# A two-layer hybrid block on one core: x loaded ahead of the weights, recurrence gates in four 64x64 quadrants, and a planner with a refitted GpSimd clock

## The chip, the cores and the metric

The kernel runs on one core of one Trainium2 chip, as one program and one launch. The metric is the time of an execution in microseconds (us), the median of several. The engines are TensorE (PE for its matmuls, PEld for its weight loads), VectorE (DVE), ScalarE (ACT), GpSimd (POOL) and SyncE (SP), which issues most of the DMAs. Each engine takes its own instructions in the order in which the program lists them, and waits on semaphores for the others. The program is laid out ahead of time: what stands in front of what on each engine is fixed when the kernel is built.

## The reference

The input is a latent stream `x` (256 tokens by 1024), 256 context tokens, two conditioning vectors, and the weights of two layers, all in float32. Each layer modulates both streams, multiplies them by one large input matrix, runs four token mixers on the result, merges their outputs, and ends with a convolutional feed-forward part.

```python
for i in range(DEPTH):                       # two layers
    mod_l = silu(c) @ w_mod[i] + b_mod[i]    # the same for the context
    zl = split_cols(modulate(x, sh1, sc1) @ w_in[i])
    zc = split_cols(modulate(h_ctx, csh1, csc1) @ w_in[i])
    ret_c, ret_l = retention(zc, zl)
    hg_c, hg_l   = hgrn2(zc, zl)
    gd_c, gd_l   = gdn(zc, zl)               # a unit lower triangular solve per 64-token chunk
    lr_c, lr_l   = rglru(zc, zl)
    y_l = merge([ret_l, hg_l, gd_l, lr_l], zl['merge_gate'])
    x = layernorm(alpha * x + g1 * y_l)
    x = layernorm(alpha * x + g2 * conv_ffn(modulate(x, sh2, sc2)))
    # the context stream does the same in every layer but the last

def rglru_direction(xc):                     # xc: conv of 512 channels, 8 blocks of 64
    r  = sigmoid(einsum('btnk,nkj->btnj', xb, w_a) + b_a)
    gi = sigmoid(einsum('btnk,nkj->btnj', xb, w_i) + b_i)
    a  = exp(-8 * r * softplus(-lam))
    h_t = a_t * h_{t-1} + sqrt(1 - a_t**2) * gi_t * xc_t
```

The recurrence's gate matrices `w_a` and `w_i` are block diagonal: 8 blocks of 64 by 64.

## The kernel before, in words

The class `Net` writes the program. Weights stream from memory in 512 KB tiles (`wraw`, issued on SP); ACT rounds each to a high part `wH` and DVE or POOL computes the low part `wL`, so that float32 products are made of matmuls named by target: `gft` and `gtf` for the input, merge and down projections, `up` for the feed-forward part, `mg_b` for the branches. `modp` matmuls make the modulation vectors from `wraw` tiles; each result row is copied by ACT (`modrow`), turned into columns by PE (`modcp`) and used as scale and shift.

The mixers are written as Python generators ("threads"). A thread yields the engine that its next step starts on and the tiles which that step needs. Two or three lanes per layer run them one behind another: the gated delta rule (`gdn0`, `gdn1`, tiles named `gd_...`) and HGRN2 (`hg_...`) in one, the recurrence (`lru_...`) and retention (`ret_...`) in another. `ro_t` are transposes of a mixer's readout. Beside them runs the stream of projection matmuls, called gemm below.

What comes next in the program is chosen by a planner. Every written instruction is charged a modelled duration on a modelled clock of its engine (`account`, L170 on), and `pump` (L302 on) takes, again and again, the candidate with the earliest modelled start: the next step of a thread, at the time at which its tiles are ready by those clocks, or the next gemm step. So a thread's step stands on PE behind as much gemm work as the planner believes will cover the wait for its input. If the input comes later than believed, PE stands still there, since the order is fixed.

The change touches four places. **The head** (`body`): the constants `ck`, then `ctx`, then `x` are loaded through ACT's queue while SP's queue loads weight tiles; `modulate` normalises both streams (row statistics, normalised `x`, transposes `xmt`, scale and shift into `xmH` and a float32 copy `xm`, low part `xmL`). **The gates** (`lru`): for each of 4 channel blocks `b` and 2 directions `d`, two matmuls of a 128x128 weight (two 64x64 blocks on its diagonal, the rest zero) against `xc` [128, 512]. A float32 matmul is two records in the trace. **The triangular solve** (`blocks`, `prep`): PE transposes `gd_Bt`, DVE masks it, SP stores 32x32 blocks to `blk` in memory and loads them as `gd_z` [64, 1024]; POOL then runs a serial substitution of 60 small operations, called the chain below; SP stores the result to `blk` and loads it back as `gd_Z`; DVE and ACT copy it into `gd_T`; PE goes on with the transposes `gd_Tt`. There are four chains, two per layer. **The planner's numbers**: POOL's cost and the placing of what follows.

Of the kernel before, what the change touches and what calls it, by code (L numbers as in the profile page):

```python
# [45 lines left out]
SUBST = 2.0  # L46
X32_BIAS = 99
LEAD = dict(PE=0.3, ACT=0.5, DVE=0.5, POOL=0.5, SP=0.0)
LN_FIRST = 1.0

EVAC_FIRST = 2.0
# [72 lines left out]
class Net:  # L124
# [36 lines left out]
    def account(self, key, name, a, k):  # L161
        dma = name == "dma_start"
        out = k.get("out", a[0] if a else None)
        if dma:
            ins = [k.get("in_", a[1] if len(a) > 1 else None)]
        else:
            ins = [x for x in a[1:] if isinstance(x, bass.AP)] + [x for n, x in k.items() if n != "out" and isinstance(x, bass.AP)]
        n = 1
        for st, c in out.ap[1:]:
            n *= c  # L170
        c = self.clk
        on, inn = self.names(out), [y for x in ins for y in self.names(x)]
        t = max([c[key]] + [max(self.base.get(x, 0.0), self.after(self.rd, x, key)) for x in on] + [self.after(self.rdy, x, key) for x in inn])
        if not dma:

            for x in ins:
                if x.space == PSUM:
                    t = max([t] + [e for p, e in self.rd.get(x.tensor.name, {}).items() if p != key])
        by = key
        if DEBUG and key == "PE":  # L180
            cand = [(c[key], "self")] + [(self.base.get(x, 0.0), "slot " + x) for x in on] + [(e + LAT[p][key], p + " rd " + x) for x in on for p, e in self.rd.get(x, {}).items()]
            cand += [(e + LAT[p][key], p + " " + x) for x in inn for p, e in self.rdy.get(x, {}).items()]
            self.dbg_t = (t, max(cand)[1].rsplit("_", 1)[0])
        if key == "PE":
            up = lambda z: 32 if z <= 32 else 64 if z <= 64 else 128
            mode = up(ins[0].ap[0][1]), up(out.ap[0][1])
            if name == "transpose":
                d = 0.11
            elif ins[0].dtype == F32R:
                mode = 128, 128  # L190
                d = (n if n >= 256 else 4 * n) / 2400.0 + 0.0135
            else:
                d = max(4 * n / 2400.0, 0.2) + 0.01
                if out.ap[0][1] == 32:
                    d *= 0.28
            if mode != self.mode:

                self.mode = mode
                d += 0.095
            d = self.clocked(t, d)  # L200
        elif dma:
            if key == "POOL":
                c[key] = t + 1.04
            else:
                self.hw = max(t + 0.05, self.hw) + 0.45
                c[key] = self.hw
            d = out.ap[0][1] * n * 4 / DMA_RATE
            t = max(c[key] + 0.7, c["DMA"])
            c["DMA"] = t + d
            by = "DMA"  # L210
        elif key == "ACT":
            d = 0.1 + n / 1200.0 + 0.07 * max(0, len(ins) - 1)
            need = {AF.Tanh: "exp", AF.Exp: "exp", AF.Ln: "ln", AF.Sqrt: "sqrt"}.get(a[2])
            if need not in (None, self.table) and not (a[2] == AF.Exp and self.table == "ln"):
                self.table = need
                t = max(t, c[key] + 1.28)
        elif key == "DVE":
            sc = [x for x in ins[1:] if len(x.ap) == 2 and x.ap[1][1] == 1]
            e = n * 1.04e-3
            src_ps = any(x.space == PSUM for x in ins)  # L220
            if name in ("tensor_scalar", "tensor_copy") and not src_ps:
                e *= 0.5
            if name == "copy_predicated":
                e = n * 1.13e-3
            if name == "reciprocal":
                e *= 6
            if name == "tensor_tensor_scan":
                e = n * 2.1e-3
            if name == "tensor_reduce" or name.startswith("bn"):
                m = 1  # L230
                for st, cc in ins[0].ap[1:]:
                    m *= cc
                e = m * 1.04e-3
            d = 0.07 + e + 0.06 * len(sc)
            if self.port_op(name, ins, sc):
                t = self.port(key, t, d)
        else:
            d = 0.14 + n * 2.1e-3
            t = self.port(key, t, d)
        if not dma:  # L240
            c[key] = t + d
        for x in on:
            q = self.rdy.setdefault(x, {})
            q[by] = max(q.get(by, 0.0), t + d)
        for x in inn:
            q = self.rd.setdefault(x, {})
            q[by] = max(q.get(by, 0.0), t + d)
# [56 lines left out]
    def pump(self, until):  # L304

        while not until():
# [3 lines left out]
            for n, x in enumerate(self.threads):  # L310
                e, r = self.when(x)
                if r is not None:
                    c.append((max(self.clk[e], r) - LEAD[e] - (x[3] if r <= self.clk[e] and e != "PE" else 0.0), n))
            if g is not None and (not c or min(c)[0] > g):
                self.gemm_step()
                continue
# [564 lines left out]
    def modulate(self, i, half, sg, xs):  # L881
# [26 lines left out]
        for d in range(0, 8, 2):  # L908
# [12 lines left out]
            for q in range(2):  # L921
                A.activation(H[:, q, :], z[q], AF.Identity, scale=sc[q], bias=sh[q])
            for q in range(2):
                if self.clk["ACT"] + X32_BIAS < self.clk["DVE"]:
                    A.activation(x32[:, q, :], z[q], AF.Identity, scale=sc[q], bias=sh[q])
                else:
                    V.tensor_scalar(x32[:, q, :], z[q], sc[q], sh[q], op0=ALU.mult, op1=ALU.add)
# [79 lines left out]
    def body(self):  # L1007
# [13 lines left out]
        f0 = self.fa = self.fb = self.pool("f0", "right")  # L1021
        self.fw = self.pool("fw")
        xs = {}
        self.A.dma_start(self.ck, self.I["c_f32"])
        for sg, nm in ((0, "ctx"), (1, "x")):
            xs[sg] = self.tile(f0, [128, 2, 1024], F32, "f_r", "x0", 2)
            self.A.dma_start(xs[sg], self.I[nm][0].rearrange("(j p) d -> p j d", p=128))
        self.feed()
        ts = [self.spawn(self.modulate(0, 0, sg, [xs[sg][:, j, :] for j in range(2)])) for sg in range(2)]
        ct = self.spawn(self.derive())  # L1030
# [460 lines left out]
    def lru(self, inst):  # L1491
# [17 lines left out]
        for b in range(4):  # L1509
            yield lambda: inst["jobs"][2 * b].done  # L1510
            xc, w = inst["xc"][b], inst["w"][b]
            yield [xc, w]
            T = self.tile(self.l2, [128, 2, 512], F32, "lT", "lru_T", 1)
            As, XIs = [], []
            for d in range(2):
                th = []
                for ty in range(2):
                    ps = self.pmt([128, 512], "lru_gp")
                    mm(ps, w[:, d * 2 + ty, :], xc, start=True, stop=True)
                    t = self.tile(self.l2, [128, 512], F32, "lt", "lru_t", 2)  # L1520
                    hb = pd["hb"][:, ty * 8 + d * 4 + b:ty * 8 + d * 4 + b + 1]
                    A.activation(t, ps, AF.Tanh, scale=0.5, bias=hb)
# [9 lines left out]
                As.append(a_)  # L1532
                XIs.append(xi)
                if d == 0:
                    yield [xc]
            yield "ACT", [T]
            A.activation(T, T, AF.Sqrt, scale=-0.25)
            yield "DVE", [T]
# [378 lines left out]
    def gdn(self, inst, g):  # L1917
# [144 lines left out]
        def prep(seg, R):  # L2062
# [8 lines left out]
                self.S.dma_start(Z[:, :, w, :], self.diag(1, seg, w))  # L2071
            for z in (T, TT):
                V.memset(z[:, :, 0, :], 0.0)
            yield "DVE", [Z, TT, T]
            for b in range(4):
                ps = slice(32 * b, 32 * b + 32)
                V.tensor_copy(TT[ps, :, 0, ps], Z[ps, :, 0, :])
# [205 lines left out]
def _host_arrays(a, specs):  # L2283
    f = np.float32
    out = {}
# [11 lines left out]
    for i in range(DEPTH):  # L2297
# [19 lines left out]
        for d in range(2):  # L2317
            for ty, nm in enumerate(("lru_w_a", "lru_w_i")):
                for bk in range(4):
                    for q in range(2):  # L2320
                        lruw[i, 64 * q:64 * q + 64, bk, d * 2 + ty, 64 * q:64 * q + 64] = a[nm][i, d, 2 * bk + q]
    out["bm"] = a["b_mod"].reshape(DEPTH, 12, 512)
    out.update(par=par, parf=parf, nw=nw, rows=rows, lruw=lruw)
    out.update(_constants())
# [31 lines left out]
```

## Time and profile before

| | |
|---|---|
| median of 3 runs | 2199.26 us (2198.85 to 2202.68) |
| profiled execution: its own time | 2195.15 us |
| profiled execution: span from first to last instruction | 2193.4 us |
| PE busy | 2023.3 us (92%) |
| DVE busy | 1478.5 us (67%) |
| ACT busy | 849.5 us (39%) |
| POOL busy | 436.4 us (20%) |
| mean TensorE clock granted | 0.967 of full speed |

PE is the engine that is hardly ever free: the span less its busy time leaves 170 us. Idle time of the other engines costs nothing by itself; it matters where PE waits for them. Times in the rows are microseconds from the start of the span. Since matmul ends are modelled and pipelined, the distance from one start to the next says more than the duration of one.

### The profile page before, as it was taken

How to read it: one execution, taken by the hardware profiler on the slowest of the kernel's cores; microseconds unless marked ns; L12 is line 12 of the kernel's file. 1: busy time of each engine (PE TensorE's matmuls, PEld its weight loads, DVE VectorE, ACT ScalarE, POOL GpSimd, SP SyncE). 2: the span in 40 equal slices, each digit the busy share in tenths (PEclk: the TensorE clock that was granted, in tenths of full speed). 3: DMA queues.
4: the chain of work that ended last, by engine and by line, in shares of the span. 5: the costliest groups of instructions: out<-in, count | busy, mean ns of one | idle time of the engine just before them, and what ended most of it. 6: DMA issues, size and time to landing. Idle time of an engine off the chain costs nothing. (4 is left out here: it accounts for less than half of the span.)

```text
span 2193.4 us, 34754 instructions
## 1 busy us (share of the span) xinstructions
PE 2023.3 (92%) x13820; PEld 1752.4 (80%) x13820; DVE 1478.5 (67%) x2491; ACT 849.5 (39%) x1259; POOL 436.4 (20%) x440
## 2 busy tenths in 40 slices
PE   5998999999999999779999997999989899888997
PEld 3676777788888878678898876788988799878996
DVE  5785665445737457986636678896584566878786
ACT  3354431322332333344423433566332333325553
POOL 0273216111101101220000022282127112301000
PEclk9999999999999999989999998999999899988999
DMA  7453434434341457553233244354433322575553
GB/s 264 130 160 100 158 112 149 134 109 142 102 150 62 159 192 254 184 192 116 92 102 97 96 149 160 126 179 133 140 107 110 112 81 75 177 272 211 181 185 115
DMA packets 128963, 316.22 MB, mean 144 GB/s; under 512 B 28928, under 2 KB 51232, under 8 KB 128800
## 3 DMA queue, kind: packets, MB, share of 16 engines
q1 hardware_dynamic: 127280, 308.96, 43.0%
q0 software_dynamic: 832, 2.54, 0.3%
q8 instruction: 109, 1.79, 0.3%
q10 hardware_dynamic: 688, 2.49, 0.3%
q14 instruction: 54, 0.44, 0.1%
HBM read 290.84 MB, written 23.10 MB: 143 GB/s over the span
## 5 line engine op out<-in xcount | busy, mean ns | idle before, releaser
L91 DVE TENSOR_TENSOR wL<-wraw,wH 128x1024 fp32r<-128x1024 f32 (+1 forms) x326 | 405.5, 1250 | 154.7 <-ACT wH L91 154.5
L91 ACT ACTIVATE wH<-wraw 128x1024 fp32r<-128x1024 f32 (+2 forms) x391 | 401.7, 1032 | 233.9 <-PE gtf L91 146.0
L91 POOL TENSOR_TENSOR wL<-wraw,wH 128x1024 fp32r<-128x1024 f32 (+1 forms) x65 | 148.2, 2284 | 1131.6 <-ACT wH L91 1078.5
L91 PE MATMUL gft<-xmH,wH 128*128 128x512 f32 x512 | 211.0, 412 | 0.8 <-ACT wH L91 0.8
L91 PE MATMUL gft<-xmL,wH 128*128 128x512 f32 x512 | 203.4, 397 | 3.7 <-DVE xmL L91 3.7
L91 PE MATMUL gft<-xms,wH 128*128 128x256 f32 x1344 | 186.6, 290 | 4.2 <-ACT wH L91 4.1
L91 PEld LDWEIGHTS gft<-xms,wH 128*128 128x128 f32 x1344 | 170.5, 193 | 11.5 <-issue 5.0
L91 DVE SCALAR_TENSOR_TENSOR ffy<-up,parf,ffy 128x255 f32<-128x255 f32 (+1 forms) x188 | 110.8, 590 | 71.3 <-ACT ffy L91 65.5
L91 PE MATMUL up<-xmL,wH 128*128 128x512 f32 (+1 forms) x400 | 146.9, 374 | 6.9 <-DVE xmL L91 6.9
L91 PE MATMUL up<-xmH,wH 128*128 128x512 f32 (+1 forms) x400 | 146.0, 372 | 5.1 <-ACT wH L91 2.8
L91 PE MATMUL gft<-xmH,wL 128*128 128x512 f32 x512 | 132.8, 398 | 0.0
L91 PEld LDWEIGHTS gft<-xmH,wH 128*128 128x128 f32 x512 | 97.5, 190 | 28.9 <-issue 8.6
L91 PE MATMUL gtf<-wH,xmH 128*128 128x256 f32 (+1 forms) x384 | 110.2, 314 | 9.0 <-DVE gy L91 7.5
L91 ACT ACTIVATE ffy<-up,parf 128x256 f32<-128x256 f32 (+1 forms) x94 | 61.3, 652 | 145.7 <-PE up L91 145.6
L91 PEld LDWEIGHTS gft<-xmL,wH 128*128 128x128 f32 x512 | 97.7, 191 | 23.6 <-DVE xmL L91 5.3
L91 PE MATMUL gtf<-wH,hidH 128*128 128x256 f32 (+1 forms) x352 | 114.3, 341 | 2.3 <-DVE gy L91 1.7
L91 PE MATMUL gtf<-wH,hidL 128*128 128x256 f32 (+1 forms) x352 | 113.9, 340 | 0.0
L91 PEld LDWEIGHTS gft<-xmH,wL 128*128 128x128 f32 x512 | 95.5, 190 | 20.0 <-issue 0.3
L91 PE MATMUL gtf<-wH,xmL 128*128 128x256 f32 (+1 forms) x384 | 105.7, 302 | 0.0
L91 PE MATMUL gft<-xms,wL 128*128 128x256 f32 x672 | 95.8, 288 | 6.1 <-DVE wL L91 6.1
L91 PE MATMUL up<-xms,wH 128*128 128x256 f32 x704 | 94.0, 287 | 5.1 <-DVE xms L91 3.8
L91 PEld LDWEIGHTS up<-xmL,wH 128*128 128x128 f32 x400 | 78.6, 197 | 20.1 <-DVE xmL L91 8.3
(330 smaller groups left out, 4272.9 us busy)
## 6 DMA issues: line engine op xcount, KB each, us to landing
wraw<-in_wt SPq DMA_DIRECT2D x466, 512.0 KB, 3.7
thd<-mg_t SPq DMA_DIRECT2D x32, 256.0 KB, 2.3
mg_th<-thd SPq DMA_DIRECT2D x32, 256.0 KB, 3.1
lnw<-in_rows SPq DMA_DIRECT2D x8, 512.0 KB, 7.1
thd<-mg_t SPq DMA_DIRECT2D x32, 128.0 KB, 2.6
xmm<-thd SPq DMA_DIRECT2D x16, 256.0 KB, 5.5
wraw<-in_wt SPq DMA_DIRECT2D x14, 256.0 KB, 2.6
brd<-ro_b SPq DMA_DIRECT2D x28, 128.0 KB, 1.9
```

The lines of the kernel that those rows point to most:

```text
L91: r = f(*a, **k)
```

## The change

First, in the head, `ctx` is loaded by SP ahead of the weight tiles, `x` is the first load on ACT's queue, and `ck` comes behind it. In the first `modulate` the float32 copies `xm` may be made by ACT where its modelled clock is behind DVE's, which puts one of each two on ACT.

Second, in `lru`, ACT makes `xs`, a copy of `xc` with its two halves of 64 partitions exchanged (two activations of [64, 512] per `b`, 16 in all). The two gates of a direction are then four matmuls of a 64x64 weight block against 64 partitions of `xc` or `xs`, one for each quadrant of the 128x128 array, in place of two matmuls of 128x128. The packed weights of the second gate are exchanged to match. There are 64 such matmuls of 64x512 in place of 32 of 128x512.

Third, the planner: POOL's modelled cost changes from 0.14 + 2.1e-3 n to 0.22 + 2.0e-3 n (n elements per partition), a step that begins on PE is placed 0.8 us later outside the head (`PE_MARGIN`), and the copies behind a chain are placed 2 us later (`CHAIN_LAG`). A 64x64 matmul is charged 0.27 of its former cost.

```diff
+PE_MARGIN = 0.8
+CHAIN_LAG = 2.0
...
                 if out.ap[0][1] == 32:
                     d *= 0.28
+                elif out.ap[0][1] == 64 and ins[0].ap[0][1] == 64:
+                    d *= 0.27
...
-            d = 0.14 + n * 2.1e-3
+            d = 0.22 + n * 2.0e-3
...
-                    c.append((max(self.clk[e], r) - LEAD[e] - (x[3] if r <= self.clk[e] and e != "PE" else 0.0), n))
+                    m = PE_MARGIN if e == "PE" and r > self.clk[e] - PE_MARGIN and not self.head else 0.0
+                    c.append((max(self.clk[e], r + m) - LEAD[e] - (x[3] if r <= self.clk[e] and e != "PE" else 0.0), n))
...
-                if self.clk["ACT"] + X32_BIAS < self.clk["DVE"]:
+                if self.clk["ACT"] + (0.0 if first else X32_BIAS) < self.clk["DVE"]:
...
+        for sg, nm, q in ((0, "ctx", self.S), (1, "x", self.A)):
+            xs[sg] = self.tile(f0, [128, 2, 1024], F32, "f_r", "x0", 2)
+            q.dma_start(xs[sg], self.I[nm][0].rearrange("(j p) d -> p j d", p=128))
         self.A.dma_start(self.ck, self.I["c_f32"])
-        for sg, nm in ((0, "ctx"), (1, "x")):
-            xs[sg] = self.tile(f0, [128, 2, 1024], F32, "f_r", "x0", 2)
-            self.A.dma_start(xs[sg], self.I[nm][0].rearrange("(j p) d -> p j d", p=128))
...
-            yield [xc, w]
+            xs = self.tile(self.l2, [128, 512], F32, "lxs", "lru_xs", 1)
+            yield "ACT", [xc, xs]
+            for q in range(2):
+                A.activation(xs[64 * q:64 * q + 64, :], xc[64 - 64 * q:128 - 64 * q, :], AF.Copy)
+            yield [xs, w]
...
+                pp = [self.pmt([128, 512], "lru_gp") for _ in range(2)]
+                for q in range(2):
+                    for ty, z in enumerate((xc, xs)):
+                        o0, i0 = 64 * q, 64 * (q ^ ty)
+                        mm(pp[ty][o0:o0 + 64, :], w[i0:i0 + 64, d * 2 + ty, o0:o0 + 64], z[i0:i0 + 64, :], start=True, stop=True)
                 for ty in range(2):
-                    ps = self.pmt([128, 512], "lru_gp")
-                    mm(ps, w[:, d * 2 + ty, :], xc, start=True, stop=True)
+                    ps = pp[ty]
...
-            yield "DVE", [Z, TT, T]
+            yield "DVE", [Z, TT, T], "free", CHAIN_LAG
...
-                        lruw[i, 64 * q:64 * q + 64, bk, d * 2 + ty, 64 * q:64 * q + 64] = a[nm][i, d, 2 * bk + q]
+                        r = 64 * (q ^ ty)
+                        lruw[i, r:r + 64, bk, d * 2 + ty, 64 * q:64 * q + 64] = a[nm][i, d, 2 * bk + q]
```

The three pieces below show how the written order moves. The first is the start of ACT's program, before and after; `ck`, `x_118` (context) and `x_120` (latents, `x_119` after) are the loads named above.

```order
L91 ACTIVATE cth<-c_91 128x16
L91 DMA ck<-in_c_f 128x768
L91 DMA x_118<-in_ctx 128x2x1024
L91 DMA x_120<-in_x 128x2x1024
L91 ACTIVATE sp_e_141<-sp_ax_140 128x8
```

After the change the same engine begins:

```order
L94 ACTIVATE cth<-c_91 128x16
L94 DMA x_119<-in_x 128x2x1024
L94 DMA ck<-in_c_f 128x768
L94 ACTIVATE sp_e_141<-sp_ax_140 128x8
L94 ACT_TABLE_LOAD
```

`x` has moved from third to first on this queue. The load of the context has gone from it and stands on SP between `par` and the first `wraw`.

The second place is PE at the end of the first chain of layer 0, from the last gemm matmuls ahead of `gd_Tt` on; `gd_Y`, `gd_X` and `gd_XT` are the next steps of the same solve. Before:

```order
L91 MATMUL gft<-xmL,wH 128x512
L91 MATMUL gd_Tt<-ck,gd_T 128x128 x8
L91 MATMUL gft<-xmH,wH 128x512
L91 MATMUL gft<-xmL,wH 128x512
L91 MATMUL gft<-xmH,wH 128x512
L91 MATMUL gft<-xmL,wH 128x512
L91 MATMUL gd_Y<-gd_T,gd_B 128x128 x4
L91 MATMUL gft<-xmH,wL 128x512 x4
L91 MATMUL gd_X<-gd_Ys,gd_T 128x2x32 x8
L91 MATMUL gd_XT<-gd_T,gd_Ys 128x128 x4
```

After, at the same place of the solve:

```order
L94 MATMUL gd_Tt<-ck,gd_T 128x128 x8
L94 MATMUL gft<-xmH,wH 128x512
L94 MATMUL gft<-xmL,wH 128x512
L94 MATMUL gft<-xmH,wH 128x512
L94 MATMUL gft<-xmL,wH 128x512
L94 MATMUL gft<-xmH,wH 128x512
L94 MATMUL gft<-xmL,wH 128x512
L94 MATMUL gft<-xmH,wH 128x512
L94 MATMUL gft<-xmL,wH 128x512
L94 MATMUL gd_Y<-gd_T,gd_B 128x128 x4
L94 MATMUL lru_gp<-lru_x,lru_w 64x512
L94 MATMUL lru_gp<-lru_xs,lru_w 64x512
```

Eight gemm matmuls in place of four stand between `gd_Tt` and `gd_Y`, and eight 64x512 gate matmuls (two shown) in place of four gemm matmuls between `gd_Y` and `gd_X`. In the stretch ahead of this piece, from the last `gd_Bt` of the chain to `gd_Tt`, the order counts 196 `gft` and 8 `lru_gp` matmuls before, 180 and 16 (of 64x512) after. For the fourth chain, in layer 1, these counts of `gft` are 244 and 144; for the second they are 92 and 200 while the shorter `gtf` go from 156 to 12; the third has 504 and 532 of the short `gft` and 12 and 16 `lru_gp`.

The third place is SP at the start of the fourth chain: the stores of `gd_Bt` to `blk` and the load of `gd_z`. Before, from the store of the last blocks on:

```order
L91 DMA thd_11537<-mg_t 128x256
L91 DMA brd_0_11533<-ro_b 128x256
L91 DMA blk_1_0_14743<-gd_Bt 128x4x32 x2
L91 DMA thd_11537<-mg_t 128x256
L91 DMA wraw<-in_wt 128x1024
L91 DMA gd_z<-blk_1_0_14743 64x1024
L91 DMA thd_11537<-mg_t 128x256
```

After:

```order
L94 DMA blk_1_0_15165<-gd_Bt 128x4x32 x4
L94 DMA wraw<-in_wt 128x1024
L94 DMA gd_z<-blk_1_0_15165 64x1024
L94 DMA ret_tab_15523<-in_c_ret 128x384
L94 DMA ret_tab_15524<-in_c_ret 128x384
L94 DMA thd_11565<-mg_t 128x256
```

The stores of all four block sets now stand together and no store of a readout (`brd`) or gate (`thd`) stands between them and the load.

## Rows read from the trace of the kernel before

**Rows 1.** The page's first part: busy time, share, instructions; and the view of cores.
```profile
PE 2023.3 (92%) x13820; PEld 1752.4 (80%) x13820; DVE 1478.5 (67%) x2491; ACT 849.5 (39%) x1259; POOL 436.4 (20%) x440
...
core 0: 2193.4 us, clock 0.967
```

**Rows 2.** Waits of PE, whole span: us in total, times, longest us.
```profile
PE gd_Tt L91 <- DVE gd_T L91: 14.8, 3, 8.8
PE modcp L91 <- ACT modrow L91: 12.0, 5, 9.6
PE ro_t L91 <- DVE ret_ob L91: 9.6, 7, 2.3
PE ro_t L91 <- DVE ro_n L91: 8.3, 4, 4.3
PE gd_Y L91 <- ACT gd_T L91: 5.7, 4, 2.8
PE hg_s L91 <- DVE hg_k L91: 5.3, 7, 2.0
PE gd_Bt L91 <- DVE gd_B L91: 4.5, 5, 1.6
PE hg_s L91 <- DVE hg_Q L91: 2.7, 2, 1.5
```

**Rows 3.** Timeline of PE, head: start, us, engine, operation, [idle before, releaser].
```profile
14.70 1.08 PE L91 MATMUL modp<-wraw,cz 128*32 128x128 f32 x16 [1.50 <-DMA wraw<-in_wt]
25.36 0.47 PE L91 MATMUL modcp<-ck,modrow 128*128 128x128 f32 x1 [9.58 <-ACT modrow L91]
30.46 1.97 PE L91 MATMUL xmt<-ck,x 128*128 128x128 f32 x16
```

**Rows 4.** Timeline of ACT, head.
```profile
3.62 0.69 ACTq L91 DMA_DIRECT2D x<-in_x  x1
23.91 1.24 ACT L91 ACTIVATE x<-x,ln_nb,rq_n 128x1024 f32<-128x1024 f32 x1 [11.66 <-DMA wraw<-in_wt]
25.05 0.26 ACT L91 ACTIVATE modrow<-modp 128x128 f32<-128x128 f32 x1
```

**Rows 5.** Timeline of DVE, head.
```profile
18.05 3.66 DVE L91 BATCH_NORM_STATS2 bst<-x 128x6 f32<-128x512 f32 x6 [3.22 <-DMA x<-in_x]
```

**Rows 6.** Windows: stretch, us, busy (x) by engine, PEclk, DMA share, GB/s.
```profile
4.00:26.00 22.00, 4.96 (x72) 2.83 (x76) 12.95 (x66) 8.00 (x13) 0.00 (x0) 1.00 1.02 406
```

**Rows 7.** Timeline of PE: gates, 64-row and 128-row matmuls side by side.
```profile
96.00 1.13 PE L91 MATMUL gd_pk<-gd_kq 64*128 64x256 f32 x8
...
212.90 1.98 PE L91 MATMUL gft<-xmH,wL 128*128 128x512 f32 x8
...
216.83 0.64 PE L91 MATMUL modp<-wraw,cz 128*32 128x128 f32 x16
...
223.02 1.88 PE L91 MATMUL lru_gp<-lru_x,lru_w 128*128 128x512 f32 x4
224.74 1.04 PE L91 MATMUL gd_Tt<-ck,gd_T 128*128 128x128 f32 x8
```

**Rows 8.** The tile lru_gp: engine, operation, duration min/median/max ns, starts.
```profile
L91 PE MATMUL lru_gp<-lru_x,lru_w x64: 590/592/697, 117.7 to 1517.5; 128*128 128x512 f32 x64
L91 ACT ACTIVATE lru_t<-lru_gp,hb x32: 665/687/691, 118.8 to 1519.3; 128x512 f32<-128x512 f32 x32
```

**Rows 9.** Timeline of PE, first and fourth chain, from gd_Bt to gd_Tt.
```profile
110.11 0.55 PE L91 MATMUL gd_Bt<-ck,gd_B 128*128 128x128 f32 x3 [1.65 <-DVE gd_B L91]
...
178.90 1.12 PE L91 MATMUL gd_Tt<-ck,gd_T 128*128 128x128 f32 x4 [8.84 <-DVE gd_T L91]
...
1635.62 0.55 PE L91 MATMUL gd_Bt<-ck,gd_B 128*128 128x128 f32 x3 [0.93 <-DVE gd_B L91]
...
1691.54 1.20 PE L91 MATMUL gtf<-wH,xms 128*128 128x256 f32 x8
...
1701.10 2.06 PE L91 MATMUL gd_Tt<-ck,gd_T 128*128 128x128 f32 x8 [5.00 <-DVE gd_T L91]
```

**Rows 10.** Timeline of POOL: first operation of the first and fourth chain.
```profile
121.68 0.24 POOL L91 TENSOR_TENSOR gd_x<-gd_z 64x30 f32<-64x30 f32 x1 [12.44 <-DMA gd_z<-blk]
...
1652.97 0.24 POOL L91 TENSOR_TENSOR gd_x<-gd_z 64x30 f32<-64x30 f32 x1 [12.49 <-DMA gd_z<-blk]
```

More of the change, by code (lines that the diff above doesn't have):

```diff
@@ L1534, in lru @@
                 if d == 0:
-                    yield [xc]
+                    yield [xs]
             yield "ACT", [T]
```

## The prediction

> **What bounds the kernel now.** I read the page's busy times first. PE is busy 2023.3 of 2193.4 us, and the other engines 67% at most [rows 1]. So the time is PE's work plus PE's idle time, 170 us, and the change can only pay by lessening one or the other. Then I asked for the waits of PE over the whole span. The reader is to see that no single wait is large: the longest kinds that the change can reach are the head's `modcp` (9.6 of 12.0 us in one piece), the transposes `gd_Tt` behind the POOL chains (8.8 and 5.0 us in two pieces), and many waits of 0.5 to 2 us in the mixers' steps, each behind a small DVE or ACT operation [rows 2]. The timelines of the head and of two chains came last, to see what those waits hang on. The clock is 0.967 of full speed on the mean [rows 1], so the lower of its two levels (1.2 against 2.4 GHz) has about 7% of the span; some of its stretches stand behind long waits, as the eight `gd_Tt` of the fourth chain, 2.06 us after 5.00 idle, against 1.04 us for eight that came without a wait [rows 7, 9].
>
> **The head.** PE is idle from the end of the fourth `modp` group (14.70 + 1.08) to 25.36 [rows 3]. It waits for `modrow`, a short ACT copy at 25.05. ACT was not busy: it had stood 11.66 us, and the copy was queued behind a normalisation of `x` [rows 4]. That needed row statistics, which began on DVE when `x` had landed, at 18.05 [rows 5]; `x` was issued at 3.62 on ACT's queue, behind the constants and the context [rows 4]. All this time the transfer engines were full, 406 GB/s at share 1.02 between 4 and 26 us [rows 6]. With `x` and the context first, 2.1 MB at 406 GB/s take 5.2 us, so both are there at about 9.5, some 8.5 us earlier, and the normalisation is over before the first four weight tiles are multiplied. Those come later by the same 5 us, from about 11 to 20, in waits that PE had anyway. The next floor is the transfer: the order of PE in the head is unchanged, and ahead of `xmt` it needs nine weight tiles of 0.52 MB, the two streams and `ck` (0.4 MB), 7.3 MB or 18 us from 4 on: 22. It started at 30.46 [rows 3]. I take 8 us; the bounds are 4 (ACT's and DVE's steps queue in another way) and 10. The half of `xm` that goes to ACT may give 1 or 2 us of the waits behind `xmL`; it is left at nothing inside these bounds.
>
> **The gates.** Four records of `lru_gp` (two matmuls) began at 223.02 and the next operation at 224.74, so they cost 1.72 us, 0.43 a record [rows 7]. There are 64 records [rows 8], 16 groups of 1.72: 27.5 us. After the change a group is eight records of the same 512 columns on a quarter of the array each. Whether quadrants run side by side no row shows for this shape. The nearest rows do for other parts: eight 64-row records of 256 columns (`gd_pk`) occupy PE from 96.00 to 97.06 at the next start, 1.13 with the last one's tail, where one by one at the gates' rate (0.43 for 512 columns) they would take 1.7; sixteen records of 32 columns of weights (`modp`) take 0.64, against 1.04 for eight full ones [rows 7]. So two halves of the rows run together, and four quarters of the columns do nearly. I take four at a time: two passes of 0.43, 0.88 us a group with the start-up, 13.4 us saved. The bounds are 27.5 us lost (eight in a row) and 13.5 saved. The sixteen half-height copies on ACT have as their nearest row 0.69 us for the 512 columns of `lru_t` [rows 8]: 11 us together, on an engine that is busy 39% [rows 1]; they lie ahead of a gate step that PE reaches with gemm work in between, and cost nothing unless that cover is short, then two copies, 1.4 us, for each of the 8 blocks at most.
>
> A rule speaks against the full gain. In the rows, the pairs that run together (`gd_pk`) come from two row halves [rows 7]. In the change, the quadrants of one gate come from both row halves and write one PSUM tile. The Trainium skill, "TensorEngine Tiling (Array Packing)", section "Gotcha 1: PSUM Pressure", says that different row tiles cannot access the same PSUM bank at one time. By that rule a group would run as two pairs, 1.72 us, and save nothing; it is the first rival below, and no run here shows it either way.
>
> **The small waits.** The rows for `ro_t`, `gd_Y`, `hg_s` and `gd_Bt` add up to 36.1 us in 29 waits, 1.2 each [rows 2]. The margin puts 0.8 us more gemm work ahead of every step of that kind: 29 times 0.8 is 23 us if each wait is long enough. The written order bears this out: between `gd_Tt` and `gd_Y` stand eight `gft` for four, 4 x 0.25 us more by the row of eight in 1.98 [rows 7]. Some waits are shorter than 0.8 and give less; some steps are moved by more, and there are as many again of under 0.8 in kinds that are not listed. I take 25 us, bounds 8 and 36. The price of the margin is that each lane lasts longer; at the end of layer 0's mixers early merges now stand among the last HGRN2 steps, so that PE has work there, and I cost that at nothing.
>
> **The chains.** They get worse. From `gd_Bt` to `gd_Tt` the first chain took 110.11 to 178.90, 68.8 us, of which PE waited 8.84 [rows 9]; POOL began at 121.68 [rows 10], and its 60 operations follow each other. The change alters none of these operations. The order puts less PE work beside them: 16 `gft` fewer (16 x 0.25 = 4.0 us) and four gate groups at half price (4 x 0.84 = 3.4). So the wait grows by 7.4, to about 16. In the fourth chain 100 `gft` of 256 columns go, 0.15 us each at most by the row of eight `gtf` of that size in 1.20: up to 15 us [rows 9]. There the chain may also start earlier: from `gd_Bt` at 1635.62 to POOL's start at 1652.97 were 17.3 us, against 11.6 in the first chain [rows 9, 10], and SP has fewer stores between them now. That gives back up to 5.7; net +8, bounds +2 and +15. The second chain has more cover now and loses its 1 us (14.8 less the two large ones [rows 2]); in the third half-priced gates thin the cover, +2. Together 7.4 + 8 - 1 + 2 = +16 us; bounds 0 and +30. `CHAIN_LAG` doesn't prevent it, since it moves the copies by 2 us in the plan, and what counts is the PE work left in front of `gd_Tt`.
>
> **The sum.** -8 - 13.4 - 25 + 16 = -30.4 us on the profiled execution's 2195.15 us (span 2193.4 and 1.75 outside): 2164.8. That execution is 4.1 us below the median of the runs, 2199.26, so by the median it is 2169. I forecast 2168 us.
>
> **The rivals.**
> 1. The quadrants of one gate exclude each other and the groups keep 1.72 us. For it: no row shows two row halves writing one PSUM tile; against it: every packed shape in the rows does gain. Sum -8 + 0 - 25 + 13 (the gates thin no cover now) = -20: 2175 to 2180.
> 2. The margin doesn't do what it says: each step is placed later, its successors too, and the same waits return because the late input is itself made by the step before. For it: the longest of the kinds are 1.5 to 4.3 us, far over the margin [rows 2], and hang on a DVE that is busy 67% [rows 1]; against it: the extra matmuls in the order. The small waits then give 5 instead of 25: -8 - 13.4 - 5 + 16 = -10: 2187 to 2190.
> 3. The slower side: the POOL chains. With less work beside them, `gd_Tt` waits at all four, by 9 + 15 + 5 more, each followed by a stretch at the lower clock (1.0 us lost on eight transposes [rows 7, 9], some 2 us a time, 6 in all), while the lengthened lanes leave the end of the mixers without gemm work and take back the small waits. Sum -8 - 13.4 + 0 + 35 = +14: about 2212. It decides from the point at which the chains' growth exceeds the 21 us of head and gates and the small waits give nothing. For it: the counts in the order; against it: only 14.8 us of waits there now. Gates run one by one (+27) would end there too.
>
> **How the numbers follow.** Forecast 0.55, the first rival 0.17, the second 0.15, the third 0.13 (with the gates in a row). The forecast's own bounds, its terms varied one or two at a time, are 2145 to 2185. The rivals reach from 2175 to 2212; I close the range at 2200, which leaves out most of the third, and at 2142 below: 2142 to 2200. A measurement of this kernel can tell about 0.2%, 4.4 us, from no change. Faster by more than that 0.83 (forecast, the first rival and most of the second), within it 0.06, slower 0.11.
>
> **What would show it.** Head: `modcp`'s wait in front of the second modulation group under 3 us, `xmt` near 22 instead of 30. Gates: eight records of a group starting within 0.9 us of each other's group; two pairs of starts 0.43 apart in 1.7 us would be the first rival. Small waits: the rows of `ro_t`, `gd_Y`, `hg_s` and `gd_Bt` down from 36 to about 11. Chains: `gd_Tt` up from 15 to about 31, nearly all in the first and fourth. The prediction is wrong if `gd_Tt` stays at 15 or less (then the plan's cover is better than the counts say, and the time is near 2150), or if PE's idle time doesn't fall.

## The result, and the profile after

The changed kernel takes 2214.97 us (median of 6 runs, 2213.43 to 2217.02), the kernel before 2201.31 us in the 6 runs beside it: a ratio of 1.0061, 95% interval 1.0050 to 1.0073. It is 13.7 us slower where 31 us faster were forecast, and lies outside the range. The third rival's price (2212) came near, but by luck: its mechanism, longer waits of `gd_Tt` at all four chains, isn't what the trace shows.

First the page's first part and the view of cores of the changed kernel, which answer to [rows 1]:

```profile
PE 2018.5 (91%) x13884; PEld 1754.1 (79%) x13884; DVE 1482.4 (67%) x2476; ACT 862.5 (39%) x1283; POOL 430.5 (19%) x447
...
core 0: 2215.2 us, clock 0.956
```

PE's busy time is 4.8 us less, its span 21.8 us more. So PE idles 27 us longer, and its clock is lower by 1.1%. Part of the 21.8 is the choice of executions: the one profiled here is the slowest of its kernel's six, and that of before was faster than all three in its table. The waits of PE after, whole span (us in total, times, longest), against [rows 2]:

```profile
PE modp L94 <- DMA wraw<-in_wt: 27.7, 14, 12.0
PE gft L94 <- ACT wH L94: 25.2, 8, 11.4
PE modcp L94 <- ACT modrow L94: 14.2, 7, 6.0
PE gd_Tt L94 <- DVE gd_T L94: 12.5, 3, 11.1
PE ro_t L94 <- DVE ret_ob L94: 12.5, 4, 5.2
PE ro_t L94 <- DVE ro_n L94: 10.0, 5, 5.7
PE gd_Bt L94 <- DVE gd_B L94: 6.4, 4, 2.5
PE hg_s L94 <- DVE hg_k L94: 4.9, 7, 1.6
...
PE gd_Y L94 <- DVE gd_T L94: 3.1, 1, 3.1
```

The kind that grew most had this row before:

```profile
PE gft L91 <- ACT wH L91: 5.0, 4, 3.4
```

The reader is to see three things. The transposes behind the chains don't wait longer in sum (12.5 for 14.8), but one of them waits 11.1 instead of 8.8. The small waits of `ro_t`, `gd_Y`, `hg_s` and `gd_Bt` add up to 36.9 us, as they did before (36.1), where the prediction had them fall to 11. And a kind that was small before has grown by 20 us: projection matmuls that wait for a rounded weight tile, 25.2 for 5.0, of which 11.4 in one piece. The largest row, `modp` behind a weight tile (20.5 us before), has its 12.0 at the very start of the head: the first tile now comes behind the two streams, as the prediction said it would.

In the head, the timeline of PE and ACT after (start, us, operation, idle before and its releaser) answers to [rows 3, 4]:

```profile
21.40 0.47 PE L94 MATMUL modcp<-ck,modrow 128*128 128x128 f32 x1 [4.00 <-ACT modrow L94]
27.22 1.97 PE L94 MATMUL xmt<-ck,x 128*128 128x128 f32 x16
36.60 0.48 PE L94 MATMUL modcp<-ck,modrow 128*128 128x128 f32 x1 [5.97 <-ACT modrow L94]
37.12 0.79 PE L94 MATMUL gft<-xmH,wH 128*128 128x512 f32 x1
...
57.16 0.80 PE L94 MATMUL gft<-xmH,wH 128*128 128x512 f32 x1 [5.35 <-ACT wH L94]
```
```profile
20.96 0.22 ACT L94 ACTIVATE lbe<-lbe 128x16 f32<-128x16 f32 x1 [2.29 <-DVE lbe L94]
21.08 0.26 ACT L94 ACTIVATE modrow<-modp 128x128 f32<-128x128 f32 x1
...
27.91 1.02 ACT L94 ACTIVATE xmH<-xmt,modc 128x256 fp32r<-128x256 f32 x2 [2.12 <-PE xmt L94]
29.54 0.56 ACT L94 ACTIVATE xm<-xmt,modc 128x256 f32<-128x256 f32 x1 [0.61 <-DVE xm L94]
...
36.28 0.27 ACT L94 ACTIVATE modrow<-modp 128x128 f32<-128x128 f32 x1
```

`xmt` starts 3.2 us earlier than before (27.22 for 30.46), not 8: `modrow` again stands behind another ACT operation, now `lbe`, whose input DVE makes only after the row statistics (DVE's timeline has those from 9.46 to 19.95, so the first of the streams was there when the prediction said). Then ACT converts two `xmH`, waits 0.61 us for DVE's `xm` of the same `xmt` tile, converts one `xm`, and so on four times: from 27.91 to 36.28, and only then `modrow`. The first projection starts at 37.12, later than before, when it began at 35.64. The second stream's conversions alternate in the same way, and PE then stands 5.35 us for `wH` at 57.16.

The third chain shows the largest new wait. Timeline of SP, ACT and PE after, near the chain's end:

```profile
1498.86 1.50 SPq L94 DMA_DIRECT2D wraw<-in_wt  x2
1516.39 0.46 SPq L94 DMA_DIRECT2D blk<-gd_z  x1
1516.94 1.22 SPq L94 DMA_DIRECT2D thd<-mg_t  x2
```
```profile
1505.81 1.05 ACT L94 ACTIVATE wH<-wraw 128x1024 fp32r<-128x1024 f32 x1
1520.24 0.38 ACT L94 ACTIVATE mg_t<-gft 128x256 f32<-128x256 f32 x1 [13.38 <-DMA thd<-mg_t]
1520.53 1.05 ACT L94 ACTIVATE wH<-wraw 128x1024 fp32r<-128x1024 f32 x1
```
```profile
1521.63 5.81 PE L94 MATMUL gft<-xms,wH 128*128 128x256 f32 x32 [11.36 <-ACT wH L94]
```

SP's queue stands 15.9 us in front of the store of the finished chain (`blk<-gd_z`). Behind it are the stores of `mg_t`; ACT can't overwrite that buffer before they are done, and `wH` is next on ACT. So a late chain stops the weight stream of PE, two engines further on. Before, SP stood in front of this store too, but a weight load was next behind it and no store of `mg_t`.

The gates do run four at a time. Timeline of PE after, first group:

```profile
119.63 0.64 PE L94 MATMUL lru_gp<-lru_x,lru_w 64*64 64x512 f32 x1
119.64 0.64 PE L94 MATMUL lru_gp<-lru_xs,lru_w 64*64 64x512 f32 x1
119.65 0.64 PE L94 MATMUL lru_gp<-lru_x,lru_w 64*64 64x512 f32 x1
119.65 0.64 PE L94 MATMUL lru_gp<-lru_xs,lru_w 64*64 64x512 f32 x1
120.11 0.59 PE L94 MATMUL lru_gp<-lru_x,lru_w 64*64 64x512 f32 x1
```

Four records start within 0.02 us and the next four 0.48 later; sixteen records without a wait take 1.88 us, where eight took 3.43 before. Over the whole span the sixteen groups take 19.3 us for 27.8, since in four of the eight pairs of groups the second starts late or the records run slower: 8.5 us saved, not 13.4. Two row halves write one PSUM tile here at one time, and the first rival falls. The Trainium skill, "TensorEngine Tiling (Array Packing)", "Gotcha 1: PSUM Pressure", says that different row tiles can't access the same PSUM bank at one time; the trace differs from it for these quadrants, whose two row halves write different partitions of the tile.

### The profile page after: what moved, and what is told of

Its sections match the earlier page's. It is cut to its first block, busy times and chain, and to the rows that moved or that the text cites. A ratio compares the mean times of both kernels' runs of the same rounds, so it can differ in the third digit from the quotient of the medians.

```text
span 2215.2 us, 34889 instructions
## 1 busy us (share of the span) xinstructions
PE 2018.5 (91%) x13884; PEld 1754.1 (79%) x13884; DVE 1482.4 (67%) x2476; ACT 862.5 (39%) x1283; POOL 430.5 (19%) x447
## 5 line engine op out<-in xcount | busy, mean ns | idle before, releaser
L94 DVE TENSOR_TENSOR wL<-wraw,wH 128x1024 fp32r<-128x1024 f32 (+2 forms) x335 | 413.9, 1242 | 168.9 <-ACT wH L94 168.6
L94 POOL TENSOR_TENSOR wL<-wraw,wH 128x1024 fp32r<-128x1024 f32 (+2 forms) x56 | 132.6, 2370 | 1069.9 <-ACT wH L94 966.1
L94 PE MATMUL gft<-xms,wH 128*128 128x256 f32 x1344 | 188.7, 294 | 19.9 <-ACT wH L94 15.9
L94 PEld LDWEIGHTS gft<-xms,wH 128*128 128x128 f32 x1344 | 175.1, 199 | 25.4 <-ACT wH L94 17.5
```

The lines of the kernel that those rows point to most:

```text
L94: r = f(*a, **k)
```

## The experiments

Each kernel ran beside the kernel before on the same chip; the medians of the latter were 2201.5 (e1 to e4), 2202.1 (e5 to e8), 2201.8 (e9 to e12), 2203.2 (e13 to e16) and 2202.3 (e17, e18). Ratios are to it, with 95% intervals; they are not the quotients of the medians and differ from them by up to 0.2%, some 4 us. "In the old order" means that the planner was charged as in the named kernel, so that all other instructions stay where they were.

**e1, e2: the head alone.** e1 issues the loads in the new order, e2 also gives half of the `xm` to ACT:

```diff
+            e.dma_start(xs[sg], src[sg])       # ctx on SP, x on ACT
+        self.nc.scalar.dma_start(self.ck, self.I["c_f32"])
...
+                elif first and q == 1:         # e2 only
+                    self.nc.scalar.activation(x32[:, q, :], z[q], AF.Identity, scale=sc[q], bias=sh[q])
```

> Before, with the two stream loads issued first (ctx on SP ahead of the weights, x first on ACT, ck behind it) and every engine's other instructions in the old order, xm all on DVE. Theory A (the loads give what the changed kernel's trace shows up to xmt, 27.2 instead of 30.5 us, and the xm half on ACT is what eats it): xmt near 27, first gft near 32.5 instead of 35.6, time 3 to 4 us below before (2197). Rival 1 (my forecast's term): 8 us below (2193). Rival 2 (a modrow or weight wait takes all of it back): within 1 us of before.

> As e1_head_loads, and one of each two xm conversions of the first layer's first modulation made by ACT. Theory A (ACT's xm waits for DVE's xm of the same tile, so ACT's eight xmH last 8.5 us instead of 3.75 and hold back modrow and wH): first gft near 37 us, 4 to 6 us slower than e1_head_loads, so 1 to 2 us above before. Rival (the split is harmless or helps): the same as e1_head_loads or 1 us below it.

Measured: e1 2199.70 us (0.9981, 0.9968 to 0.9994), e2 2204.77 (1.0009, 0.9995 to 1.0023). In e1 `xmt` starts at 26.92 and the first projection at 32.11; in e2 at 26.40 and 36.29. The loads are worth 2 us by the medians and 4 by the ratio, and the half of `xm` on ACT costs 5.

**e3: the gates alone, in the old order.**

```diff
+            for q in range(2):
+                self.nc.scalar.activation(xs[64 * q:64 * q + 64, :], xc[64 - 64 * q:128 - 64 * q, :], AF.Copy)
...
+                        self.nc.tensor.matmul(pp[ty][o0:o0 + 64, :], w[i0:i0 + 64, d * 2 + ty, o0:o0 + 64], z[i0:i0 + 64, :], start=True, stop=True)
+                    self.account("PE", "matmul", (ps, w[:, d * 2 + ty, :], xc), dict(start=True, stop=True))
```

> Before, with the gates in four 64x64 quadrants and the ACT copies xs, all other instructions of every engine in the old order. Theory A (eight records take 0.9 instead of 1.72 us, 13 us of PE work less, of which the first and third chains take back some 3 us each because less work stands in front of gd_Tt): 6 to 10 us below before, gd_Tt behind the first chain waits 11 to 12.5 instead of 8.8. Rival (the stretches are bound by DVE and the POOL chain, so PE's saved work turns into waits): within 2 us of before.

Measured: 2211.53 us (1.0025, 1.0005 to 1.0045), against both theories. Its ten runs lie between 2197.2 and 2215.0 and go with their clock: the shortest has 0.968 granted, the longest two 0.959 and 0.960. Which of the two, time or clock, makes the other isn't shown.

**e4: the planner's three numbers alone**, as in the change.

```diff
+            d = 0.22 + n * 2.0e-3
+                    m = 0.8 if e == "PE" and r > self.clk[e] - 0.8 and not self.head else 0.0
+            yield "DVE", [Z, TT, T], "free", 2.0
```

> Before, with the planner's three numbers alone (POOL cost 0.22 + 2.0e-3 n, PE_MARGIN 0.8, CHAIN_LAG 2.0). Theory A (the new placing is what loses the time: stores of chains and retention readouts that stand in front of other engines' work): 10 to 25 us above before, 2212 to 2226. Rival 1 (my forecast: small waits shrink by 25, chains grow): 5 to 25 us below. Rival 2 (the numbers alone are harmless, the loss comes from the three parts planned together): within 4 us of before.

Measured: 2187.80 us (0.9918, 0.9899 to 0.9936). My theory that the new placing loses the time is wrong; it gains 14 us by the medians (18 by the ratio). It doesn't gain them as forecast: in its trace the small waits are still 33.0 us, and `gd_Tt` has fallen from 14.8 to 2.7.

**e5, e6: the change without its gates; the change without its head.**

```diff
+                    mm(ps, w[:, d * 2 + ty, :], xc, start=True, stop=True)    # e5: as before, no xs
...
+                if self.clk["ACT"] + X32_BIAS < self.clk["DVE"]:             # e6, and loads as before
```

> The changed kernel with the gates back to two full 128x128 matmuls: head and planner's numbers. Theory B (the numbers gain 14 alone, the gates are what turns the plan: cheap gate steps leave PE with less work in front of late inputs): about the sum of the runs so far, head with xm +3 and numbers -14, so 2188 to 2194. Rival (the head's changed clocks are what turns the plan): stays at 2208 to 2216. Rival 2 (any new plan scatters by some 10 us): anywhere between.

> The changed kernel with the head as before (loads and xm): gates and planner's numbers. Theory B (the gates turn the plan): stays slow, 2205 to 2213, with PE's waits behind wH in the third chain and behind ret_ob in layer 1 as in the changed kernel. Rival (the head turns it): 2180 to 2190. If the gates were worth their 8.5 us of PE time beside the numbers: 2179.

Measured: e5 2188.28 us (0.9937, 0.9919 to 0.9956), e6 2211.19 (1.0039, 1.0022 to 1.0056). The loss comes with the gates: with the same head and numbers, e5 is 14 us below the kernel before and the changed kernel 14 above, 27 us apart. PE idles 30.8 us less in e5's trace (165.9 for 196.7), and these two rows, 25.2 and 12.5 in the changed kernel, have most of that:

```profile
PE gft L94 <- ACT wH L94: 10.4, 6, 5.3
PE gd_Tt L94 <- DVE gd_T L94: 2.5, 1, 2.5
```

The two long waits shown above, 11.36 at the third chain and 11.1 at the first, are not there. Ahead of the first chain's `gd_Tt` e5's trace has 220 `gft` where the changed kernel has 180, so PE has more gemm work in front of it there.

**e7, e8: the numbers with e1's loads; the change with POOL's cost moved by 1%.**

```diff
-            d = 0.22 + n * 2.0e-3
+            d = 0.222 + n * 2.0e-3
```

> Before with the planner's numbers and the stream loads first, in the order that the numbers alone give, xm on DVE, gates as before. If the parts add at a fixed order: 2 to 4 us below the numbers alone, about 2184 to 2186, the fastest so far. Rival (the head's gain is lost in the first waits of the mixers): 2188.

> The changed kernel with POOL's cost at 0.222 instead of 0.22 per operation, a change of 1% in one constant, which moves some 340 rows of PE's order. Theory C (the loss is an accident of one plan): leaves the changed kernel's 2215 by 8 us or more in either direction. Theory B: within 5 us of it.

Measured: e7 2181.33 us (0.9902, 0.9872 to 0.9932); the two gains add within the noise. e8 2203.14 (1.0008, 0.9993 to 1.0022), 12 us below the changed kernel, and neither long wait is in its trace (5.3 us at most behind `wH`, 1.6 in front of `gd_Tt`). So a part of that kernel's loss is an accident of one plan, and a difference of 12 us between two plans doesn't by itself show a cause.

**e9, e10: e3's edit on e7, in e7's order; the change with another price of the gates in the plan.** e10's edit:

```diff
-                    d *= 0.27
+                    d *= 0.5
```

> e7_planner_head with the gates in quadrants and the copies xs, every other instruction in e7's order (the plan still charges two full matmuls). Theory B1 (the gates lose only through the plan that their price makes): their 8.5 us of PE time show, 2172 to 2177. Theory B2 (they lose where they run: the copies on ACT stand in front of weight conversions, and PE at half the array after a wait): 2184 to 2192, slower than e7's 2181.

> The changed kernel with the planner's price of a 64x64 matmul at 0.5 instead of 0.27 of its old price, so that four cost as much as two full ones; the instructions are the same, their order is not (in front of the first chain's gd_Tt 200 gft and 20 gate matmuls instead of 180 and 16, in front of the fourth 216 gft instead of 144). Theory B1 (price and plan): 2180 to 2192, gd_Tt behind the first chain waits under 5 us instead of 11. Theory B2 (the gates lose where they run): 2205 to 2215.

Measured: e9 2194.33 us (0.9961, 0.9943 to 0.9978), 13 us above e7; e10 2198.39 (0.9982, 0.9970 to 0.9994), 17 below the changed kernel. e9 is as the second theory said; e10 lies between the two. The gates lose 13 where they run, in e7's order (6 to 10 in the order of before, e3). At their price the plan loses up to 17: e10's trace has neither long wait (`gd_Tt` 0.4 and `gft` behind `wH` 10.1 us in all, as in e5), but a new plan alone gave 12 (e8), so what is the price's own lies between 5 and 17. e9's trace shows where a part of the first goes. Timeline of ACT, then of PE, at the end of its first chain:

```profile
174.21 1.26 ACT L91 ACTIVATE gd_T<-gd_Z 32x128 f32<-32x128 f32 x4 [8.25 <-DMA gd_Z<-blk]
175.48 1.27 ACT L1521 ACTIVATE lru_xs<-lru_x 64x512 f32<-64x512 f32 x2
```
```profile
167.33 1.07 PE L1530 MATMUL lru_gp<-lru_x,lru_w 64*64 64x512 f32 x2
176.80 1.11 PE L1530 MATMUL lru_gp<-lru_xs,lru_w 64*64 64x512 f32 x1 [8.40 <-ACT lru_xs L1521]
178.71 1.94 PE L91 MATMUL gd_Tt<-ck,gd_T 128*128 128x128 f32 x8
```

At the same place PE's timeline in e7 has:

```profile
169.62 1.88 PE L91 MATMUL lru_gp<-lru_x,lru_w 128*128 128x512 f32 x4
174.28 1.93 PE L91 MATMUL gd_Tt<-ck,gd_T 128*128 128x128 f32 x8 [2.78 <-DVE gd_T L91]
```

In e9 ACT waits 8.25 us for the chain's result, and the copies `xs` are next in its queue. Full gates needed only `xc` and could run while the chain ended; these wait for it, and `gd_Tt` stands behind them. The changed kernel has no such wait: there the plan knows of the copies, and no gate stands for `lru_xs` in its rows.

**e11, e12: the margin alone; POOL's cost and `CHAIN_LAG` alone.**

```diff
+                    m = 0.8 if e == "PE" and r > self.clk[e] - 0.8 and not self.head else 0.0   # e11
...
+            d = 0.22 + n * 2.0e-3                              # e12
+            yield "DVE", [Z, TT, T], "free", 2.0               # e12
```

> Before with PE_MARGIN 0.8 alone. My forecast's terms: the small waits give, the chains aren't helped: if the margin is what gains, 2185 to 2190 and gd_Tt still waits 10 or more in all. Rival (the gain of the numbers is the chains' alone): within 3 us of before, 2199 to 2204.

> Before with POOL's refitted cost and CHAIN_LAG 2.0, no margin. If the chains' waits are what the numbers remove (gd_Tt from 16.6 to 4 us in the trace of the numbers alone): 2186 to 2192. If the margin gains it: 2196 to 2203.

Measured: e11 2186.13 us (0.9931, 0.9910 to 0.9952), e12 2207.99 (1.0029, 1.0018 to 1.0041), the latter outside both theories. The margin makes the gain. In e12 `gd_Tt` waits only 0.5 us and the kernel is 6 us slower than before; so a shorter wait behind the chains doesn't by itself shorten the run. Waits of PE in e11:

```profile
PE gd_Tt L91 <- DVE gd_T L91: 10.4, 2, 9.6
PE ro_t L91 <- DVE ret_ob L91: 7.7, 4, 6.2
PE hg_kt L91 <- DVE hg_k L91: 5.0, 1, 5.0
PE ro_t L91 <- DVE ro_n L91: 4.5, 4, 1.4
PE hg_s L91 <- DVE hg_k L91: 3.8, 5, 1.6
PE gd_Bt L91 <- DVE gd_B L91: 3.2, 4, 1.5
```

`ro_t`, `hg_s` and `gd_Bt` have 19.2 us where [rows 2] have 30.4, and `gd_Y` (5.7) no longer waits; `hg_kt` with 5.0 is new. That is 17 us less in these kinds, but PE's idle time is only 5 us less than before (165.1 for 170.1), since other kinds have grown. So the rows bear out where the margin acts, and don't account for all of the 15 us.

**e13, e14: e9 with the copies made by DVE behind `lru_x`; e9 without copies** (the second gate reads the wrong half, so that part of the result is left out).

```diff
+                for q in range(2):             # e13, in the job that makes xc
+                    self.nc.vector.tensor_copy(xs[64 * q:64 * q + 64, :], xc[64 - 64 * q:128 - 64 * q, :])
```

> e7_numbers and head loads with the gates in quadrants as in e9, all other instructions in e7's order, but the copies xs made by DVE directly behind the operation that makes lru_x. Theory D (the copies' place behind ACT's wait for the chain is what loses): lru_gp waits for nothing near the first chain, the gates' 8.5 to 12 us show, 2169 to 2176. Rival (the quadrants or DVE's 6 us of copies lose it): 2184 or more.

> As e9_numbers_head_gates without the copies: the second gate's matmuls read xc in place of xs, so the second gate is computed from the wrong half. Theory D: 2168 to 2175, like e13. Rival (the matmuls on quarters of the array lose, as by a lower clock behind them): stays at 2188 to 2197 like e9.

Measured: e13 2189.23 us (0.9941, 0.9920 to 0.9961), e14 2187.03 (0.9926, 0.9906 to 0.9946). Both miss theory D's time. The copies' place costs about 5 of the 13 us by e13, where the two intervals overlap, and 7 by e14. The gain doesn't come even without any copy: in e14 the gates take 11 us less PE time than in e7 (16.8 for 27.8, from start to next operation, without the waits of what follows them), yet it isn't faster, 6 us slower by the medians with intervals that overlap. Of the waits of PE these three kinds grew most, e7 first, then e14:

```profile
PE gft L91 <- POOL wL L91: 8.0, 2, 4.9
PE gft L91 <- ACT wH L91: 5.0, 6, 1.6
PE gd_Tt L91 <- DVE gd_T L91: 2.8, 1, 2.8
```
```profile
PE gft L91 <- POOL wL L91: 11.7, 3, 6.5
PE gft L91 <- ACT wH L91: 8.8, 9, 2.2
PE gd_Tt L91 <- DVE gd_T L91: 6.4, 1, 6.4
```

These three have 11.1 us more, and PE idles 8.4 us longer in all. The rest of PE's work takes 7 us longer, at a mean clock of 0.958 for 0.962. POOL's chain and the weight conversions end these stretches; most of the PE time saved beside them came back as waiting, and the slower rest made it a loss in these two traces. Whether the waits also make the lower clock was not tested; a cost of the quadrants by way of the clock stays a rival.

**e15, e16: the change with the copies on DVE, planned anew; the change with the chain's store on POOL's own queue, in its order.**

```diff
-            yield "ACT", [xc, xs]              # e15, with the two activations
+                    V.tensor_copy(xs[64 * q:64 * q + 64, :], xc[64 - 64 * q:128 - 64 * q, :])
...
-            self.S.dma_start(self.blk[1].rearrange("p i j -> p (i j)"), z)   # e16
+            dst = self.blk[1].rearrange("p i j -> p (i j)")
+            self.nc.gpsimd.dma_start(dst, z)
```

> The changed kernel with the copies xs on DVE behind lru_x, planned anew. Theory D says only that lru_gp no longer waits for lru_xs; the price of the gates still thins the cover, so 2200 to 2212. If the copies were all of it: 2185 to 2192.

> The changed kernel, every engine in its order, but the store of each finished chain issued on POOL's own queue instead of SP's, so that SP doesn't stand in front of the stores of mg_t and the weight loads until the chain ends. Theory E: the wait of gft for wH in the third chain falls from 11.4 to under 5 us, the time to 2203 to 2210. Rival (SP stands at the load of gd_Z instead, and all is as late): 2212 to 2217.

Measured: e15 2208.04 us (1.0027, 1.0013 to 1.0040), within theory D's 2200 to 2212, and e16 2212.63 (1.0044, 1.0028 to 1.0061), as its rival said and not clear of the changed kernel's interval. In e16 the wait for `wH` falls to 7.0 us and comes 10 us later: SP now stands at the load of `gd_Z` until 1524.6. SP's queue is in the path as read, but taking one of two blocking DMAs off it moves the wait more than it removes it, so what this wait costs in time isn't shown.

**e17, e18: e7 with the margin doubled; e7 with the margin and the loads alone.**

```diff
+                    m = 1.6 if e == "PE" and r > self.clk[e] - 1.6 and not self.head else 0.0   # e17
...
-            d = 0.22 + n * 2.0e-3                              # e18: back to before
-            yield "DVE", [Z, TT, T], "free", 2.0               # e18: back to before
```

> e7_planner_head with PE_MARGIN 1.6 instead of 0.8. If the margin gains by shortening the small waits, most of which are under 1.6 us: a further 3 to 8 us, 2173 to 2178. Rival (the lanes' length then shows at the end of the mixers and in the chains): 2184 to 2195.

> e7_planner_head without POOL's cost and CHAIN_LAG: the margin and the stream loads alone. If the two planner terms are worth nothing beside the margin: 2180 to 2185, e7's 2181. If they help the chains: 2186 to 2190, and gd_Tt waits some 10 us instead of 3.

Measured: e17 2215.12 us (1.0060, 1.0040 to 1.0081), e18 2178.43 (0.9888, 0.9869 to 0.9907). e17 is slower than both theories had it. e18 is the fastest kernel of the study, but its interval overlaps e7's; `gd_Tt` waits 9.6 us in it for 2.8 in e7, without making it slower. Against e11, which differs in the loads alone, it is 8 us faster. The gain doesn't grow with the margin. Waits of PE in e17:

```profile
PE ro_t L91 <- DVE ro_n L91: 22.5, 6, 5.0
PE ro_t L91 <- DVE ret_ob L91: 17.4, 4, 7.1
PE hg_s L91 <- DVE hg_k L91: 9.2, 5, 2.9
```

The waits for readouts are more than twice those of before; placed later still, the steps run out of other work to stand behind. That last half sentence is the reading of these rows and wasn't tested by itself.

## Why the prediction was wrong

**Gates: the step that failed.** "13.4 us saved" followed from PE being busy 92% of the span, as if each PE microsecond were one of time. The gates cost 27 us instead (e5 to the changed kernel). The size of the operation was nearly right: 0.94 us a group without a wait, forecast 0.88, and 8.5 us saved over the sixteen groups. But the groups lie beside the POOL chains and weight conversions, which end those stretches: without any copies 11 us of PE time gave no gain at all (e14 to e7). The prediction had the row for this, 8.84 us of waiting at the end of that very stretch [rows 9], and charged the thinner cover of the gates only 3.4 us there and 2 in the third chain.

**The copies cost nothing: failed at a fixed order.** They were covered by ACT being busy 39%. In e9 their place in ACT's queue decided, behind an operation that waits for the chain: 5 us by e13, 7 by e14. I had named that risk only as 1.4 us for each block.

**The chains: wrong in size and form.** The wait at the first chain grew by 2.3 us (8.84 to 11.14), not by 7.4. In the fourth `gd_Tt` hardly waits; the readouts of retention in the same stretch have 10.1 us (4.90 and 5.17) where they had 6.4, so the +8 didn't come. In the third the wait came through SP's queue, 11.4 us, where I had put 2; I read PE's order against POOL's chain and didn't follow what stands behind the chain's store on SP. My own sign of error, `gd_Tt` at 15 or less, did occur (12.5), but not with the 2150 us that I tied to it: the waits had moved to other kinds. The gates' price in the plan, which I listed and didn't cost, is worth up to 17 us (e10): at this price the plan can bring in both long waits (the changed kernel), though it need not (e8).

**Small waits: failed as a term.** 25 us were forecast; in the changed kernel these waits are where they were (36.9 for 36.1), and with the three numbers alone 3 us less (e4). The second rival had said that they would return. The numbers do gain 14 to 18 us, and the margin alone 15 (e11), where the kinds named do give 17; but the sum of PE's idle time follows only in part, so how the margin gains stays open. Doubled, it loses (e17), so 0.8 us can't be read as a rate.

**Head: half of its size.** At three fixed orders the first projection starts 3.5 to 4.2 us earlier with the new loads (e1, e7 and e18 against before, e4 and e11), and the medians fall by 2 to 8, for 8 forecast: the floor was ACT's queue, behind DVE's row statistics, and not the transfers. The half of `xm` on ACT, left at nothing, costs 5, since two engines read one tile in turn.

**The sum.** From runs: loads, `xm` and numbers -14 (e5), gates +27, measured 13.7. Of the 27, 13 are where the gates run (e9 to e7) and up to 17 their price in the plan (e10); these two were taken at different orders, so they needn't add up better, and e8 shows that one plan can differ from the next by 12 us. Which of the plan's decisions behind the price lose most was not taken apart beyond the waits shown.

## What to carry to other kernels

A busy share of 92% over the span doesn't make every operation of that engine worth its time: look at the wait that ends the stretch in which it stands. If a serial chain elsewhere ends it, a cheaper operation there buys a longer wait. When a change adds a helper on an idle engine, read what stands in front of it in that engine's queue, and what work loses its independence by needing it. In a kernel whose order comes from modelled costs, a change of price is a change of the whole program: time it apart from the change of the instructions, and time a neighbouring price too. A kind of wait that shrinks isn't yet time gained: look at the engine's idle time as a whole.

## What the runs showed of the hardware

Four float32 matmuls on 64x64 quadrants run side by side although two row halves write the same PSUM tile, each its own partitions (0.02 us from first to fourth start, 0.94 us for eight records of 512 columns, against 1.72 before for the same gates). And the same program in one order can spread by 18 us with its clock (e3: span 2195.4 at a mean of 0.968, 2213.3 at 0.959).
